# W_out and y land in the ring of keys and queries during the last pair of heads

## The chip, the cores and the metric

The kernel runs on one core of one Trainium2 chip. A core has TensorE (PE, with its weight loads listed as PEld), VectorE (DVE), ScalarE (ACT), GpSimd (POOL) and SyncE (SP), whose queue sends the DMAs of this kernel; PSUM holds the sums of matmuls, SBUF all other tiles. The metric is the device time of one execution in microseconds; lower is better. The kernel before takes 1277.64 us, the median of three runs (1276.83 to 1278.07).

## What is computed

A trunk of two layers on a sequence of 1024 tokens with 1024 channels. Layer 0 mixes by causal pooling, layer 1 by "forgetting" attention with 16 heads of 64 channels; both add a small attention into 256 memory tokens, and each ends with an output projection and a layer norm:

```python
def mixer_sublayer(x, mem, w_in, w_mem_kv, w_out, main_fn):
    h = x @ w_in
    ...
    y_main = main_fn(u_main)
    y_mem = memory_attention(q_mem, mem, w_mem_kv)
    y = jnp.concatenate([y_main * jax.nn.silu(g_main), y_mem * jax.nn.silu(g_mem)], axis=-1)
    return y @ w_out
...
    x = layer_norm(ALPHA * x + y, ln_g[layer], ln_b[layer])
```

In layer 1 `main_fn` is `softmax(q k / 8 + cum[t] - cum[s])` over the causal keys, times the values. The change lies in the last two of its 16 heads.

## The kernel before

**Precision.** A product of float32 numbers is done as three products of halves: `hi_lo` (line 138) copies a tile to its rounded high part on ScalarE and subtracts it on VectorE to get the low part; `gp_hi_lo` (144) does both on GpSimd. A matmul group is then hi*hi, hi*lo, lo*hi.

**Slabs.** `slab` (170) computes 128 channels of a projection for all tokens: 48 matmuls of 512 columns in two pieces of 24, each piece with weights of 256 KB. `split_w` (148) fetches a piece into a tile of the ring "raw" (`raw`, 113: four buffers, shared by all weight pieces) and splits it into two tiles of the ring "w" (six buffers, so three pieces). From the attention on, `low[0]` is set and GpSimd does this split.

**Attention.** `fox` (793) runs the 16 heads in pairs; `hd` is the head, `i` runs over eight query tiles, from the longest (eight blocks of keys) down to one. One turn of this loop is called a step in what follows, and in pair 7 (heads 14 and 15) the code numbers it itself: `step = b * ST + i`, 0 to 15. A step does, in this order: the logits of its tile on PE into one or two buffers of the PSUM ring "L" (`probs`, 695; GpSimd first masks the diagonal block of the head's row `R`, line 707); bias and row minimum on VectorE (715); the exponential on ScalarE (723); then for the step before it the split of the probabilities into two halves (744, 745), which a transposing DMA (754) turns; part of the filling work; the values' products of the tiles that are five steps old (`LAG`), two tiles at a time (`values`, 756); and the rest of the filling.

**Filling.** `Fill` holds generators of slab matmuls, and `pump` lets them out by the column, so that PE always has work between the dependent parts. In pair 7 the filling is four slabs of gates: pair 7's own, then `late_gate` (784) for pairs 3, 5 and 6, twelve matmuls a step. A late gate loads the pair's output `o` back from memory into the ring "R" (two buffers, shared with the rows of the heads), and GpSimd multiplies it by the gate in four parts (790) and stores it.

**Order.** PE's instructions keep the order of the program (`manual_schedule`). Those of the other engines are laid out by the framework's planner; a tile's buffer is handed out from its ring when one is free, and all semaphores are made from that. `hi_lo` with `pinned` keeps its two instructions at their place in the program. Each engine, and SP's queue too, works its instructions in order.

**The output projection.** `OutProj` (337) handles W_out as 24 pieces of [128, 512] (256 KB each), in the order of `KKS`, two neighbours sharing a pair of tiles (hi and lo) that `wtile` hands out from the rings named in `wtags` (866). `fetch(upto)` sends pieces into raw buffers, `split(upto)` splits them. Eight pieces are fetched and split in pair 7, by two lists over the 16 steps: fetched up to (0, 0, 1, 2, 3, 4, 5, 6, 6, 6, 7, 7, 7, 8, 8, 8), split up to (0, 0, 0, 1, 2, 3, 4, 5, 6, 6, 6, 6, 7, 7, 8, 8). `early` (383) brings the memory part of y (chunk 2) for the first 256 tokens through two raw buffers (sent at steps 9 and 12, split at steps 11 and 15) and then multiplies it with these eight pieces, 48 matmuls that fill the five steps of "head 16", in which only the last values are left. `rest` (395) splits pieces 8 to 23, and goes through the remaining products and the norms.

**The ring "B"** (`xy`, 539) has ten buffers of 4 KB per partition. Each pair of heads takes six of them, three to a head: its queries, its keys and the keys with halves swapped. Before, W_out's tiles in pair 7 come from "MK" (pieces 0 and 1), "V" (2 and 3) and "B" (4 to 7), and y's two halves from "B". The tiles of the exponential's input (`p` in `probs`) also come from "MK", which has four buffers.

Of the kernel before, what the change touches and what calls it, by code (L numbers as in the profile page):

```python
# [9 lines left out]
F32 = mybir.dt.float32  # L10
# [8 lines left out]
P = 128  # L19
# [4 lines left out]
NH = 512  # L24
HEADS = 16
# [46 lines left out]
def trunk_kernel(ctx, tc, x, xT, memT, win, wk, wv0, wv, wmk, wmv, wout, poolw, pscale, lng, lnb, bforget, out):  # L72
# [5 lines left out]
    nc = tc.nc  # L78
# [15 lines left out]
    def nm(tag):  # L94
        count[0] += 1
        return f"{tag}{count[0]}"

    def sb(shape, tag, bufs, dt=F32, where=None):
        return (where or pool).tile(shape, dt, tag=tag, name=nm(tag), bufs=bufs)
# [4 lines left out]
    def G(shape=(P, S), dt=F32):  # L104
        return sb(list(shape), "G", 4, dt)
# [7 lines left out]
    def raw(shape):  # L113
        return sb(list(shape), "raw", 4)
# [7 lines left out]
    def w_slots(tags, where):  # L122

        def tiles(k):
            tag, bufs = tags[k]
            if tag == "w":
                return [[wt([P, NH]) for _ in range(2)] for _ in range(2)]
            if tag == "MK":
                pair = [MK([P, 2, NH]) for _ in range(2)]
            elif tag == "PG":  # L130
                pair = [sb([P, 2, NH], "P", 4, F32R), sb([P, 2, NH], "G", 4, F32R)]
            else:
                pair = [sb([P, 2, NH], tag, bufs, F32R, where) for _ in range(2)]
            return [[t[:, j, :] for j in range(2)] for t in pair]

        return tiles

    def hi_lo(hi, lo, src, pinned=False):

        pin = tc.keep_in_program_order if pinned else lambda ins: ins  # L140
        pin(nc.scalar.copy(hi, src))  # L141
        pin(nc.vector.tensor_tensor(lo, src, hi.bitcast(F32), ALU.subtract))  # L142
# [117 lines left out]
    def gate_units(w_dram, dst, XH, XL):  # L260
        return slab(w_dram, XH, XL, lambda cols, acc: gate(acc, dst[:, cols]))
# [75 lines left out]
    class OutProj:  # L337
# [4 lines left out]
        def __init__(self, l, wtile, yd):  # L342
            self.l, self.wtile, self.yd, self.ws, self.accs = l, wtile, yd, [{}, {}], None
            self.raws, self.n = [], 0

        def fetch(self, upto):

            while self.n + len(self.raws) < upto:
                n = self.n + len(self.raws)
                r = raw([P, NH])  # L350
                nc.sync.dma_start(r, wout[self.l, n // 2 % 2, 2 * self.KKS[n // 4] + n % 2])
                self.raws.append(r)
# [27 lines left out]
                            )  # L380
                            yield NH

        def early(self, yh, yl):


            for j in range(2):
                r, two = raw([P, 2, 2 * P]), slice(2 * j, 2 * j + 2)
                nc.sync.dma_start(r, self.yd[2, :, two, : 2 * P])
                yield
                hi_lo(yh[:, two, :], yl[:, two, :], r, True)  # L390
                yield
            self.accs = self.open()
            yield from self.products(self.accs, 2, yh, yl)
# [79 lines left out]
    with tc.tile_pool(name="in0", bufs=1) as in0:  # L473
# [49 lines left out]
        wtags = [("B", 8)] * 4 + [("W", 4)] * 2 + [("MK", 4)] * 2 + [("Y", 4)] * 2 + [("PG", 0), ("w", 0)]  # L523
        out_proj = OutProj(0, w_slots(wtags, in0), y0d)
# [12 lines left out]
    with tc.tile_pool(name="in1", bufs=1) as in1:  # L537

        def xy(shape=(P, S)):
            return sb(list(shape), "B", 10, F32R, in1)  # L540

        def vt(shape, dt=F32R):
            return sb(shape, "V", 4, dt, in1)
# [121 lines left out]
        def pair_units(p):  # L665

            yield from qk_units(p)
            if p >= 2:
                u = MK([P, S], F32)
                yield from slab(wv[p - 2], XH, XL, lambda cols, acc: nc.scalar.copy(u[:, cols], acc))  # L670
            pairs[p].append(first_vs[p] if p < 2 else values_of(u))
# [18 lines left out]
        def forget_rows(hd):  # L690
            R = sb([P, S], "R", 2, F32, in1)
            nc.sync.dma_start(R, cumd[hd].partition_broadcast(P))
            return R
# [90 lines left out]
        def late_gate(pr):  # L784
            o, g = sb([P, S], "R", 2, F32, in1), G()
            nc.sync.dma_start(o, y1d[pr // 4, :, pr % 4, :])
            yield from gate_units(win[1, 12 + pr], g, XH, XL)
            for c in range(4):
                cols = slice(c * 2 * P, (c + 1) * 2 * P)
                nc.gpsimd.tensor_tensor(o[:, cols], o[:, cols], g[:, cols], ALU.mult)  # L790
            nc.sync.dma_start(y1d[pr // 4, :, pr % 4, :], o)

        def fox(following, out_proj):
            fill, past, fresh = Fill(), [None] * LAG, [None]
            gs = {}

            def gate_ahead(pr):
                gs[pr] = G()
                fill.add(gate_units(win[1, 12 + pr], gs[pr], XH, XL), SLAB)

            ahead_R = forget_rows(0)
            for hd in range(HEADS + 1):
                pr, b = divmod(hd, 2)
                if hd == HEADS:
                    fill.add(lead, SLAB)
                if hd < HEADS:
                    if b == 0:
                        o, sums = G(), sb([P, 4 * ST], "sums", 2, F32, small).rearrange("p (n b i) -> p n b i", n=2, b=2)
                        if 0 < pr < 7:
                            fill.add(pair_units(pr + 1), 3 * SLAB)  # L810
                        for ahead in {0: (0, 1), 2: (2,), 4: (4,), 7: (7,)}.get(pr, ()):
                            gate_ahead(ahead)
                            if ahead == 0:
                                fill.add(following, SLAB)
                        for late in (3, 5, 6) if pr == 7 else ():
                            fill.add(late_gate(late), SLAB)
                    R, ahead_R = ahead_R, None
                for i in range(ST if hd < HEADS else LAG):
                    tile_of = ST - 1 - i
                    ahead = sum(SHARE[i:]) + (sum(SHARE) if b == 0 else 0)  # L820
                    part = fill.left * SHARE[i] / (ahead if hd < HEADS else sum(SHARE[i:LAG]))
                    new, split = None, []

                    def inverse():
                        if fresh[0]:
                            old, k, es, of = fresh[0]
                            fresh[0] = old, k, es, inverse_of(old, k, len(es), of)

                    def behind():
                        if fresh[0]:  # L830
                            split.append(halves(*fresh[0]))
                            fresh[0] = None

                    if i == 2 and hd < HEADS - 1:
                        ahead_R = forget_rows(hd + 1)
                    if pr == 7:
                        step = b * ST + i
                        out_proj.fetch((0, 0, 1, 2, 3, 4, 5, 6, 6, 6, 7, 7, 7, 8, 8, 8)[step])
                        if step == 9:
                            lead = out_proj.early(*(xy((P, 4, 2 * P)) for _ in range(2)))  # L840
                        if step in (9, 12):
                            next(lead)
                    if hd < HEADS:
                        new = (hd, tile_of, o)
                        fresh[0] = probs(hd, tile_of, R, sums, inverse, behind)
                    else:
                        inverse()
                        behind()
                    if pr == 7:
                        out_proj.split((0, 0, 0, 1, 2, 3, 4, 5, 6, 6, 6, 6, 7, 7, 8, 8)[step], True)  # L850
                        if step in (11, 15):
                            next(lead)
                    fill.pump(part * FRAC[0])
                    for what in split:
                        turn(*what)
                    older = past[0]
                    if older and older[1] % 2 == 0:
                        values(older[0], older[1] // 2, older[2])
                        if older[0] % 2:
                            pair_out(older[0] // 2, older[1] // 2, older[2], gs.get(older[0] // 2))  # L860
                    fill.pump(part * (1 - FRAC[0]))
                    past = past[1:] + [new]
                if b or hd == HEADS:
                    fill.pump(float("inf"))

        wtags = [("MK", 4), ("V", 4)] + [("B", 10)] * 4 + [("w", 0), ("MK", 4), ("R", 2), ("V", 4), ("PG", 0), ("B", 10)]
        out_proj = OutProj(1, w_slots(wtags, in1), y1d)
        with tc.manual_schedule(engines={PE}):
            own, following = pair_units(0), pair_units(1)
# [66 lines left out]
```

## Time and profile before

The table is of the profiled execution; "busy" is time in which an engine executes.

| | us |
|---|---|
| median of the runs | 1277.64 |
| the profiled execution, its own time | 1276.2 |
| its span, first to last instruction | 1274.5 |
| PE busy | 1245.2 |
| DVE busy | 803.1 |
| ACT busy | 578.3 |
| POOL busy | 172.5 |

The page's second part shows the whole span in 40 slices. PE is at 9 tenths or more almost everywhere, and the granted clock (PEclk) too; each column is 31.9 us; pair 7 of the heads is in columns 34 to 36, head 16 in the 36th, the projection and the last norms in what follows.

```profile
PE   9999999999999999999999999999999998989997
DVE  6444766366455555376457888777878887654644
PEclk9999999999999999999999999999999999989998
```

In the profile's rows a line stands for an instruction or a group of equal ones: start (or nothing), duration, engine, line of the code, operation, tile written <- tiles read, count; in brackets the idle time before it and what ended that. "pj" is the PSUM ring of the slabs, "L" that of the logits, "O" that of the values, and a tile's name is its ring's. The rows in the prediction with a stretch of time ahead give its length and the busy time of PE, PEld, DVE, ACT and POOL with instruction counts, then the granted clock, the DMA share and GB/s.

### The profile page before, as it was taken

How to read it: one execution, taken by the hardware profiler on the slowest of the kernel's cores; microseconds unless marked ns; L12 is line 12 of the kernel's file. 1: busy time of each engine (PE TensorE's matmuls, PEld its weight loads, DVE VectorE, ACT ScalarE, POOL GpSimd, SP SyncE). 2: the span in 40 equal slices, each digit the busy share in tenths (PEclk: the TensorE clock that was granted, in tenths of full speed). 3: DMA queues.
4: the chain of work that ended last, by engine and by line, in shares of the span. 5: the costliest groups of instructions: out<-in, count | busy, mean ns of one | idle time of the engine just before them, and what ended most of it. 6: DMA issues, size and time to landing. Idle time of an engine off the chain costs nothing. (4 is left out here: it accounts for less than half of the span.)

```text
span 1274.5 us, 19683 instructions
## 1 busy us (share of the span) xinstructions
PE 1245.2 (98%) x7018; PEld 1035.8 (81%) x7018; DVE 803.1 (63%) x1901; ACT 578.3 (45%) x1273; POOL 172.5 (14%) x276
## 2 busy tenths in 40 slices
PE   9999999999999999999999999999999998989997
PEld 6888888888888888888887778887888786868885
DVE  6444766366455555376457888777878887654644
ACT  5233643242321123266226677766767776542110
POOL 0000000000000000000013334343333332420000
PEclk9999999999999999999999999999999999989998
DMA  6333543242453323254517686867968697784430
GB/s 228 103 100 100 124 120 121 83 124 86 158 200 106 103 82 126 75 125 107 161 51 189 134 194 154 187 164 181 185 156 179 158 197 169 159 232 172 166 115 34
DMA packets 267427, 178.66 MB, mean 140 GB/s; under 512 B 212288, under 2 KB 225728, under 8 KB 267328
## 3 DMA queue, kind: packets, MB, share of 16 engines
q1 hardware_dynamic: 267328, 177.40, 52.6%
q8 instruction: 55, 0.90, 0.3%
q14 instruction: 44, 0.36, 0.1%
HBM read 94.97 MB, written 22.61 MB: 92 GB/s over the span
## 5 line engine op out<-in xcount | busy, mean ns | idle before, releaser
L180 PE MATMUL pj<-A,w 128*128 128x512 f32 x2928 | 725.3, 395 | 10.8 <-POOL w L145 9.2
L180 PEld LDWEIGHTS pj<-A,w 128*128 128x128 f32 x2928 | 537.2, 189 | 114.9 <-POOL w L145 9.6
L142 DVE TENSOR_TENSOR w<-raw,w 128x512 fp32r<-128x512 f32 x106 | 73.6, 695 | 105.5 <-ACT w L141 104.6
L723 ACT ACTIVATE T<-MK,s 128x512 f32<-128x512 f32 x192 | 110.8, 577 | 51.6 <-DVE s L715 39.2
L141 ACT CAST w<-raw 128x512 fp32r<-128x512 f32 x106 | 65.7, 621 | 149.0 <-PE pj L180 102.8
L745 DVE SCALAR_TENSOR_TENSOR P<-T,s,P 128x512 f16<-128x512 f32 x192 | 111.8, 614 | 31.6 <-ACT P L744 29.7
L744 ACT ACTIVATE P<-T,s 128x512 f16<-128x512 f32 x192 | 102.7, 576 | 46.4 <-ACT T L723 17.6
L168 PE MATMUL L<-B,B 128*128 128x512 f32 (+3 forms) x384 | 91.3, 343 | 5.0 <-DVE s L715 4.7
L168 PEld LDWEIGHTS L<-B,B 128*128 128x128 f32 x384 | 70.3, 188 | 25.9 <-DVE s L715 12.7
L620 POOL MEMSET G<- 128x128 f32 x1 | 0.2, 204 | 609.5 <-DVE V L334 609.5
L168 PEld LDWEIGHTS <-V 128*128 128x128 f16 x1152 | 66.8, 100 | 19.4 <-issue 18.9
L715 DVE CUSTOM_DVE_ANT_0 MK<-L,R 128x512 f32<-128x512 f32 (+3 forms) x128 | 72.9, 570 | 11.7 <-PE L L168 8.2
L168 PE MATMUL O<-T,V 128*128 128x128 f16 x1152 | 77.7, 223 | 1.7 <-DVE G L771 1.7
L142 DVE TENSOR_TENSOR T<-T,T 128x1024 fp32r<-128x1024 f32 x23 | 28.1, 1222 | 68.2 <-PE L L377 50.4
L146 POOL TENSOR_TENSOR w<-raw,w 128x512 fp32r<-128x512 f32 x54 | 69.7, 1291 | 3.8
L141 ACT CAST T<-T 128x1024 fp32r<-128x1024 f32 x23 | 24.2, 1052 | 99.0 <-DMA T<-y0d 50.5
L707 POOL TENSOR_SCALAR_AFFINE_SELECT R<-R 128x128 f32<-128x128 f32 x128 | 41.1, 327 | 172.3 <-DVE s L715 150.0
L145 POOL TENSOR_SCALAR w<-raw 128x512 fp32r<-128x512 f32 x54 | 35.4, 656 | 143.4 <-PE pj L180 130.4
L213 PE MATMUL pj<-T,w 128*128 128x256 f32 x384 | 48.7, 284 | 0.9 <-DVE w L142 0.8
L213 PEld LDWEIGHTS pj<-T,w 128*128 128x128 f32 x384 | 47.6, 192 | 2.0 <-DVE w L142 1.3
L377 PE MATMUL pj<-B,T 128*128 128x512 f32 x186 | 46.5, 392 | 0.5 <-DVE T L142 0.5
L377 PE MATMUL L<-B,T 128*128 128x512 f32 x174 | 43.0, 391 | 0.0
(214 smaller groups left out, 1598.6 us busy)
## 6 DMA issues: line engine op xcount, KB each, us to landing
raw<-in_win_dram SPq DMA_DIRECT2D x96, 256.0 KB, 2.8
raw<-in_wout_dram SPq DMA_DIRECT2D x48, 256.0 KB, 2.9
B<-B SPq DMA_DIRECT2D x32, 256.0 KB, 3.9
R<-cumd SPq DMA_DIRECT2D x16, 512.0 KB, 4.4
y0d<-Y SPq DMA_DIRECT2D x12, 512.0 KB, 3.1
T<-y0d SPq DMA_DIRECT2D x12, 512.0 KB, 4.1
T<-y1d SPq DMA_DIRECT2D x11, 512.0 KB, 4.0
raw<-in_wmk_dram SPq DMA_DIRECT2D x16, 256.0 KB, 2.6
```

The costliest lines, as they stand in the source:

```text
L141: pin(nc.scalar.copy(hi, src))
L142: pin(nc.vector.tensor_tensor(lo, src, hi.bitcast(F32), ALU.subtract))
L146: nc.gpsimd.tensor_tensor(lo, src, hi.bitcast(F32), ALU.subtract)
L168: nc.tensor.matmul(acc, a, b, start=i == 0, stop=i == len(terms) - 1)
L180: nc.tensor.matmul(accs[n], a[:, k, :], b[:, kt, n * NH : (n + 1) * NH], start=kt == 0 and i == 0, stop=kt == KT - 1 and i == 2,)
L213: nc.tensor.matmul(acc, w[:, k, :], m[pc][:, k, :], start=pc == 0 and k == 0 and i == 0, stop=pc == 1 and k == 3 and i == 2,)
L377: nc.tensor.matmul(accs[a][nh], y[:, k, a * P : (a + 1) * P], w, start=kt == 8 and i == 0, stop=kt == 7 and i == 2,)
L707: nc.gpsimd.affine_select(R[:, qs], R[:, qs], [[-1, P]], ALU.is_ge, -NEG, base=0, channel_multiplier=1).ins
L715: nc.vector.tensor_tensor_reduce(p[:, lo:up], lg, R[:, lo:up], 1.0, top, ALU.add, ALU.min, m[:, n : n + 1])
L723: nc.scalar.activation(e, p[:, lo:up], AF.Exp, bias=top, scale=-1.0, accum_out=sums[:, n, hd % 2, i : i + 1],)
L744: nc.scalar.activation(pair[:, lo:up], e, AF.Copy, scale=r)
L745: nc.vector.scalar_tensor_tensor(pair[:, L + lo : L + up], e, r, pair[:, lo:up], ALU.mult, ALU.subtract)
```

## The change

Pieces of W_out and of y no longer go through raw buffers in pair 7.

- A new function `land` takes a float32 tile from the ring "B". `fetch_two` sends two neighbouring pieces of W_out into the two halves of one such tile, with one DMA for each piece. It is called at steps 0, 1, 5 and 11, which makes the eight pieces.
- `early` gets one such tile for all of y's chunk (512 KB) and loads it with one DMA at step 9 in place of two into raw buffers; the halves are split from it at steps 12 and 13 (before: 11 and 15).
- The list of splits is changed: piece 5 moves from step 8 to step 11, piece 6 from step 12 to 14, piece 7 from step 14 to 15.
- At the start of head 16, `fetch(12)` sends pieces 8 to 11 into raw buffers; before, `rest` did that.
- In `wtags` the first and third entry change places: pieces 0 and 1 are split into "B", pieces 4 and 5 into "MK".

```diff
+        def fetch_two(self, land):
+
+            n = self.n + len(self.raws)
+            for j in range(2):
+                nc.sync.dma_start(land[:, j, :], wout[self.l, n // 2 % 2, 2 * self.KKS[n // 4] + j])
+                self.raws.append(land[:, j, :])
+
...
-        def early(self, yh, yl):
-
-
-            for j in range(2):
-                r, two = raw([P, 2, 2 * P]), slice(2 * j, 2 * j + 2)
-                nc.sync.dma_start(r, self.yd[2, :, two, : 2 * P])
-                yield
-                hi_lo(yh[:, two, :], yl[:, two, :], r, True)
+        def early(self, y, yh, yl):
+
+
+            nc.sync.dma_start(y, self.yd[2, :, :, : 2 * P])
+            yield
+            for two in (slice(0, 2), slice(2, 4)):
+                hi_lo(yh[:, two, :], yl[:, two, :], y[:, two, :], True)
                 yield
...
+        def land(shape):
+            return sb(list(shape), "B", 10, F32, in1)
+
...
-                        out_proj.fetch((0, 0, 1, 2, 3, 4, 5, 6, 6, 6, 7, 7, 7, 8, 8, 8)[step])
+                        if step in (0, 1, 5, 11):
+                            out_proj.fetch_two(land((P, 2, NH)))
                         if step == 9:
-                            lead = out_proj.early(*(xy((P, 4, 2 * P)) for _ in range(2)))
-                        if step in (9, 12):
+                            lead = out_proj.early(land((P, 4, 2 * P)), *(xy((P, 4, 2 * P)) for _ in range(2)))
                             next(lead)
+                    if hd == HEADS and i == 0:
+                        out_proj.fetch(12)
...
-                        out_proj.split((0, 0, 0, 1, 2, 3, 4, 5, 6, 6, 6, 6, 7, 7, 8, 8)[step], True)
-                        if step in (11, 15):
+                        out_proj.split((0, 0, 0, 1, 2, 3, 4, 5, 5, 5, 5, 6, 6, 6, 7, 8)[step], True)
+                        if step in (12, 13):
                             next(lead)
...
-        wtags = [("MK", 4), ("V", 4)] + [("B", 10)] * 4 + [("w", 0), ("MK", 4), ("R", 2), ("V", 4), ("PG", 0), ("B", 10)]
+        wtags = [("B", 10), ("V", 4), ("MK", 4)] + [("B", 10)] * 3 + [("w", 0), ("MK", 4), ("R", 2), ("V", 4), ("PG", 0), ("B", 10)]
```

## The prediction

> **What bounds the kernel now.** I read the page's totals first, then who TensorE (PE) waits for, then busy time in stretches around the change.
>
> ```profile
> span 1274.5 us, 19683 instructions
> PE 1245.2 (98%) x7018; PEld 1035.8 (81%) x7018; DVE 803.1 (63%) x1901; ACT 578.3 (45%) x1273; POOL 172.5 (14%) x276
> ```
>
> PE is busy for 98% of the span, so the change can only pay in the 29 us where PE stands still, or where it runs slowly. Who it waits for, in us, times and longest:
>
> ```profile
> PE pj L180 <- POOL w L145: 9.2, 2, 5.5
> PE L L168 <- DVE s L715: 4.7, 11, 0.7
> PE O L168 <- DVE G L771: 1.7, 1, 1.7
> PE pj L377 <- DVE T L142: 0.5, 1, 0.5
> ```
>
> The first row is two waits of a gate's slab for its weights as GpSimd (POOL) splits them. Both lie in the last pair of heads, in the steps of that pair that I count as 6 and 14 (a step is one query tile of one head; it begins with its logits on PE, and pair 7 has steps 0 to 15). In stretches, with the granted clock and the DMA share and GB/s last:
>
> ```profile
> 1053.34:1076.22 22.88, 22.88 (x135) 18.92 (x134) 18.50 (x51) 16.19 (x36) 4.36 (x7) 1.00 0.66 144
> 1076.22:1089.31 13.09, 7.42 (x46) 5.58 (x44) 5.27 (x17) 4.52 (x11) 5.06 (x7) 0.74 0.76 188
> 1089.31:1115.15 25.84, 25.84 (x150) 21.40 (x148) 19.35 (x54) 17.77 (x42) 11.94 (x18) 1.00 0.75 169
> 1115.15:1126.58 11.43, 7.69 (x46) 5.84 (x45) 3.87 (x12) 3.78 (x10) 2.66 (x4) 0.70 0.97 226
> 1126.58:1146.05 19.47, 17.24 (x107) 13.73 (x106) 13.99 (x22) 11.63 (x22) 6.58 (x7) 1.00 0.74 229
> ```
>
> Rows one and three are steps 0 to 5 and 7 to 13: PE never pauses, VectorE (DVE, third figure) is busy 81% and 75%. Rows two and four are steps 6 and 14. They are long, and PE's clock is down to 0.74 and 0.70 in them; in all other rows it is 1.00. The order of time, on PE:
>
> ```profile
> 1076.22 0.40 PE L168 MATMUL L<-B,B 128*128 128x256 f32 x2
> 1082.15 3.00 PE L180 MATMUL pj<-A,w 128*128 128x512 f32 x5 [5.54 <-POOL w L145]
> 1089.31 0.33 PE L168 MATMUL L<-B,B 128*128 128x128 f32 x2
> 1115.15 0.40 PE L168 MATMUL L<-B,B 128*128 128x256 f32 x2
> 1119.15 3.00 PE L180 MATMUL pj<-A,w 128*128 128x512 f32 x5 [3.61 <-POOL w L145]
> ```
>
> Why POOL is late is seen from POOL, SyncE's queue (SP) and DVE, in that order:
>
> ```profile
> 1081.48 0.62 POOL L145 TENSOR_SCALAR w<-raw 128x512 fp32r<-128x512 f32 x1 [3.08 <-DMA raw<-in_win_dram]
> 1118.36 0.74 POOL L145 TENSOR_SCALAR w<-raw 128x512 fp32r<-128x512 f32 x1 [3.94 <-DMA raw<-in_win_dram]
> ...
> 1055.40 0.33 SPq L351 DMA_DIRECT2D raw<-in_wout_dram  x1
> 1077.46 0.38 SPq L150 DMA_DIRECT2D raw<-in_win_dram  x1
> 1108.25 5.49 SPq L754 DMA_TRANSPOSE T<-P  x2
> 1114.46 0.39 SPq L150 DMA_DIRECT2D raw<-in_win_dram  x1
> ...
> 1076.45 0.69 DVE L142 TENSOR_TENSOR MK<-raw,MK 128x512 fp32r<-128x512 f32 x1
> 1111.14 1.13 DVE L142 TENSOR_TENSOR B<-raw,B 128x512 fp32r<-128x512 f32 x1
> ```
>
> POOL waits for the weights' DMA, and SP sent that DMA late. The ring "raw" has four buffers. At 1055.40 the fourth piece of W_out takes the last one; nothing comes free until VectorE splits the first pieces, the second ending at 1077.14. At 1077.46 the gate's weights leave, 1.2 us after the step that needs them began. For step 14 the buffer comes free with the first half of y at 1112.27, and SP sends the load at 1114.46, after the transposes that stand before it in its queue. So raw buffers held by W_out and y are the cause of both waits.
>
> **The change, part by part.**
>
> *Raw buffers freed.* In pair 7 the ring then serves the gates' weights alone, eight pieces for four buffers, so a load can go as soon as POOL has split the piece four places ahead. What the two waits cost I take from the length of the steps, since the slow clock after each wait counts too. A step of this kind without a wait is put together from rows of the same work, start to start:
>
> ```profile
> 1046.98 0.40 PE L168 MATMUL L<-B,B 128*128 128x256 f32 x2
> 1047.21 1.09 PE L180 MATMUL pj<-A,w 128*128 128x512 f32 x4
> 1048.15 1.85 PE L168 MATMUL O<-T,V 128*128 128x128 f16 x30
> 1049.81 1.41 PE L180 MATMUL pj<-A,w 128*128 128x512 f32 x5
> ...
> 1062.53 1.33 PE L180 MATMUL pj<-A,w 128*128 128x512 f32 x5
> 1063.70 0.95 PE L168 MATMUL O<-T,V 128*128 128x128 f16 x14
> 1064.46 1.87 PE L180 MATMUL pj<-A,w 128*128 128x512 f32 x7
> 1066.17 0.75 PE L168 MATMUL L<-B,B 128*128 128x384 f32 x4
> ```
>
> Two logits of 256: 0.23 (1047.21 - 1046.98); five gate matmuls 1.17; thirty of the values 1.66; seven gate matmuls 1.71. Sum 4.77 us. Step 6 took 13.09 (1076.22 to 1089.31), so 8.32 too long: 5.54 of waiting and 2.78 of slow work behind it. Step 14 took 11.43: 6.66 too long, 3.61 and 3.05. **Removed: 14.98 us**, if both loads come in time. The lower end is 0.
>
> The Trainium skill ("TensorE: Matmul & The Clock Gate", Part 1) says that the clock halves after an idle window of about 3.4 us and is whole again after about 3.4 us of sustained work. Half clock for 3.4 us would cost 1.7 us behind each wait, and the sum would be 9.15 + 3.4 = 12.6, the time 2.4 us higher than mine. The rows decide: 13.09 x 0.26 and 11.43 x 0.30 are both 3.4 us of full clock lost, twice as much. That the 1.7 us in the third row of PE's waits (at 1143) left the clock at 1.00 agrees with the page's threshold.
>
> *Landings in the ring "B".* Ten buffers of 4 KB. Pair 7's queries and keys hold six, three of which come free when head 14 is done (step 7). By the diff: two pieces land at step 0 and two at step 1 (four free, two left); step 3 gives the first split two (none left); step 4 frees one, step 5 takes it; step 6 frees one; step 7 frees three; y, its two halves and the last two pieces take all four at steps 9 to 12; steps 11 and 13 free one each, and the split of step 14 takes these. Each buffer is free at least one step (3.8 us: six in the first stretch's 22.88) before it is wanted, with none to spare. Cost taken: 0. Upper end: a cast that waits here holds ScalarE's queue, with the exponentials behind it; if the first is late by a whole step, and PE feels it all, 3.8 us.
>
> *DMAs and SP.* Eight W_out loads of 256 KB remain eight, sent in pairs; y goes as one load in place of two, one issue less (0.38 us of SP in the row at 1077.46, of the same size). SP still waits for a buffer at the third landing, with transposes behind it. Probabilities are needed on PE five steps after they are made, some 15 to 19 us, so a wait of a few us is hidden; without that cover it would cost its length. Between -0.4 and +1, taken 0. The packets of steps 0 to 15 crowd into 15 us less: 1053.34 to 1126.58 has a mean share of 0.76 by the four rows, so 0.95 in 58 us; row four carried 0.97 on all queues.
>
> *The splits moved by a step or several* (pieces 5 to 7, halves of y) are the same instructions on ScalarE and VectorE (0.69 us each on VectorE, row at 1076.45): sum 0. Their cover changes: VectorE used the waits to catch up. How far behind was it?
>
> ```profile
> 1081.62 0.48 DVE L745 SCALAR_TENSOR_TENSOR P<-T,s,P 128x256 f16<-128x256 f32 x1 [0.59 <-ACT P L744]
> ```
>
> That is its last work of step 6, done at 1082.1; unstalled, PE would begin step 7 at 1076.22 + 4.77 = 1081.0. So VectorE keeps up to within a step, and the logits have two buffers. I add 0.5 us for short waits of "PE L <- DVE" (eleven of at most 0.7 us now); ends 0 and 2.
>
> *fetch(12) at head 16* sends four W_out pieces of the output projection before it starts, through raw buffers that now are free. That helps the end of this stretch:
>
> ```profile
> 1137.57 0.61 SPq L411 DMA_DIRECT2D T<-y1d  x1
> 1143.69 1.05 ACT L141 CAST T<-T 128x1024 fp32r<-128x1024 f32 x1 [0.22 <-DMA T<-y1d]
> 1146.05 1.20 PE L377 MATMUL pj<-B,T 128*128 128x512 f32 x4 [0.49 <-DVE T L142]
> ```
>
> Here y's first chunk waits on SP behind W_out pieces. Waits of 1.7 and 0.49 us could go (-2.2); but ScalarE and VectorE also lose the pause of step 14 in which they caught up. Taken 0, upper end in the third rival.
>
> **Sum.** The profiled execution took 1276.2 us (span 1274.5 and 1.7 around it). 1276.2 - 14.98 + 0.5 = 1261.7. The median of the runs lies 1.4 above the profiled one (1277.64 - 1276.2): **1263 us**.
>
> **Rivals.**
>
> *One of the two waits stays.* For: POOL works in order, and the late gates' products (L790) wait there for a DMA, with splits behind them; SP's transposes hold loads back (5.49 us for two). Against: with buffers free the loads and splits move ahead by steps, not by microseconds. If the second stays, 1263 + 6.7 = 1269.7; if the first, 1271.3.
>
> *The wait moves to head 16.* The chain of W_out pieces and y's first chunk ended at 1146.05. If it moves up by the first step's 8.3 us but not by the second's 6.7, PE arrives that much before it: 1263 + 6.7 = 1269.7, and with half a clock behind the wait up to 1272.7. For: raw buffers turn over only as fast as VectorE splits. Against: four pieces are there beforehand.
>
> *Slower: POOL is held by the late gates' own loads.* Step 9's mask stands on POOL behind L790, which waits for its o from memory:
>
> ```profile
> 1095.11 1.43 POOL L790 TENSOR_TENSOR R<-R,G 128x256 f32<-128x256 f32 x2 [7.42 <-DMA R<-y1d]
> 1098.94 0.29 POOL L707 TENSOR_SCALAR_AFFINE_SELECT R<-R 128x128 f32<-128x128 f32 x1
> 1100.77 0.85 PE L168 MATMUL L<-B,B 128*128 128x512 f32 x4
> ```
>
> The mask ends 1.5 us before PE's next logits. It happens twice (late gates 3 and 5). If crowded DMA makes each load longer than now by d, PE waits d - 1.5 and then 2.9 more at half clock. It decides at 2(d + 1.4) > 17, d above 7 us; at d = 8 the price is 18.8 and the time 1281.8. Against: the three loads of o differ by 1.5 us, while the DMA share went from 0.75 to 0.97:
>
> ```profile
> DMA to landing us min/median/max: 4.6/5.0/6.1
> ```
>
> *The change doesn't do what it says*: the landings' waits in "B" hold SP as the raw ones did, and the gates' loads behind them are as late: 1277.6. Against: the count of buffers above.
>
> **Numbers.** Forecast 0.60 (own range 1260.5 to 1266, from the ends -2.2 and +2 with about 1 of the others), one wait stays 0.14, moved to head 16 0.10, no effect 0.05, slower 0.11. A measurement here tells 0.2%, 2.6 us, from no change. All but the last two are faster: 0.84, same 0.05, slower 0.11. Range 1260 to 1272: it holds the first and nearly all of the next two.
>
> **What would show it.** Right: no wait of PE for POOL L145 in pair 7, the clock at 1.00 from step 0 to 15, in_win loads sent several us before their splits, steps 6 and 14 at about 4.8 us. Wrong: a wait over 3.6 us and a clock under 1.00 at another place (logits behind a mask, the projection's first matmul), ScalarE idle for a "B" buffer, or SP waiting long at a landing.

## The result and the profile after

The changed kernel takes 1264.44 us, the median of six runs (1261.06 to 1266.88), against 1277.86 us for the kernel before (1275.49 to 1280.29, six runs). The ratio is 0.9892, with a 95% interval of 0.9872 to 0.9912. The profiled execution took 1262.09 us with a span of 1260.4, 14.1 less than the one before.

Totals of the changed kernel's page (the code from line 345 on has moved down; L384 is the projection's matmul, L724 the row minimum, L779 and L780 the two instructions, on ScalarE and VectorE, that empty the values' PSUM buffer, here called their evacuation):

```profile
span 1260.4 us, 19678 instructions
PE 1241.2 (98%) x7018; PEld 1033.4 (82%) x7018; DVE 802.5 (64%) x1901; ACT 577.7 (46%) x1273; POOL 173.5 (14%) x276
```

The work is the same, to five instructions. What went is PE's waiting, and slow work behind it. Whom it waits for now in the whole span:

```profile
PE L L168 <- DVE s L724: 4.5, 11, 0.5
PE O L168 <- DVE G L780: 2.0, 1, 2.0
PE idle L92 <- DVE warm L89: 1.3, 1, 1.3
PE pj L180 <- ACT A L141: 1.1, 1, 1.1
PE pj L213 <- DVE w L142: 0.8, 1, 0.8
```

The row "PE pj L180 <- POOL w L145", 9.2 us before, is gone. Between 1040 and 1140 us only the wait of 2.0 us is left. In the same stretches as before (steps 0 to 5, step 6, steps 7 to 13, step 14, then head 16 up to the projection's first matmul with a new chunk of y):

```profile
1053.22:1076.10 22.88, 22.88 (x135) 18.91 (x134) 18.56 (x52) 15.64 (x35) 8.50 (x12) 1.00 0.83 194
1076.10:1080.87 4.77, 4.77 (x45) 4.05 (x44) 3.75 (x13) 4.69 (x13) 3.42 (x4) 1.00 0.86 218
1080.87:1106.71 25.84, 25.84 (x150) 21.39 (x148) 20.47 (x57) 17.76 (x42) 11.70 (x18) 1.00 0.98 226
1106.71:1111.48 4.77, 4.77 (x46) 4.05 (x45) 3.98 (x12) 3.27 (x9) 0.69 (x1) 1.00 1.02 221
1111.48:1131.07 19.59, 17.62 (x106) 14.30 (x105) 13.56 (x22) 11.83 (x23) 7.34 (x7) 0.94 0.71 217
```

Steps 6 and 14 take 4.77 us each, with the clock at 1.00. Steps 0 to 5 and 7 to 13 last as long as before to 0.01 us. The 16 steps took 73.24 us (1053.34 to 1126.58) and take 58.26 now: 14.98 less. The last row is the exception. Its clock of 0.94 over 19.59 us means that work worth 1.2 us at the full clock was lost, and PE waits there:

```profile
1122.89 0.62 ACT L141 CAST MK<-raw 128x512 fp32r<-128x512 f32 x1 [2.87 <-DMA raw<-in_wout_dram]
1126.33 0.62 ACT L141 CAST R<-raw 128x512 fp32r<-128x512 f32 x1 [2.81 <-DMA raw<-in_wout_dram]
1126.97 0.47 ACT L779 ACTIVATE G<-O,unscale 64x256 f32<-64x256 f32 x1
1128.30 0.49 PE L168 MATMUL O<-T,V 128*128 128x128 f16 x6 [1.97 <-DVE G L780]
1128.61 2.67 PE L384 MATMUL L<-B,B 128*128 128x512 f32 x6
```

These rows are ScalarE's and PE's in order of time. The values of tiles 3 and 2 are ready on PE at 1121.9, and a short ScalarE instruction (L779), with one on VectorE behind it, should empty their PSUM buffer. It stands in ScalarE's queue behind casts of W_out pieces 15 and 16, which wait 2.87 and 2.81 us for their loads. PE's last values wait for that buffer, and the six matmuls after the wait take 2.67 us where six of this form take 1.52.

The loads that were late before leave early now. SP's rows of the gates' weights in pair 7's neighbourhood:

```profile
1047.65 0.33 SPq L150 DMA_DIRECT2D raw<-in_win_dram  x1
...
1055.92 0.38 SPq L150 DMA_DIRECT2D raw<-in_win_dram  x1
...
1063.95 0.54 SPq L150 DMA_DIRECT2D raw<-in_win_dram  x1
```

The last of these is the second piece of late gate 6, wanted at step 14. It was sent at 1114.46 before, and is sent at 1063.95 now, 43 us ahead of its step. The raw buffers don't stay with the gates' weights, though: from 1071.46 on, in step 4, the planner sends pieces 8 to 11 of W_out into them, far ahead of the place where the program asks for them.

### The profile page after: what moved, and what is told of

Same layout as the page of the kernel before. It is cut to its first block, busy times and chain, and to the rows that moved or that the text cites. A ratio compares the mean times of both kernels' runs of the same rounds, so it can differ in the third digit from the quotient of the medians.

```text
span 1260.4 us, 19678 instructions
## 1 busy us (share of the span) xinstructions
PE 1241.2 (98%) x7018; PEld 1033.4 (82%) x7018; DVE 802.5 (64%) x1901; ACT 577.7 (46%) x1273; POOL 173.5 (14%) x276
## 5 line engine op out<-in xcount | busy, mean ns | idle before, releaser
L180 PE MATMUL pj<-A,w 128*128 128x512 f32 x2928 | 722.5, 394 | 1.2 <-ACT A L141 1.1
L180 PEld LDWEIGHTS pj<-A,w 128*128 128x128 f32 x2928 | 536.0, 188 | 104.1 <-ACT A L141 2.8
L724 DVE CUSTOM_DVE_ANT_0 MK<-L,R 128x512 f32<-128x512 f32 (+3 forms) x128 | 72.9, 569 | 9.8 <-PE L L168 6.8
L141 ACT CAST T<-T 128x1024 fp32r<-128x1024 f32 x23 | 24.2, 1051 | 98.4 <-DMA T<-y0d 49.9
L145 POOL TENSOR_SCALAR w<-raw 128x512 fp32r<-128x512 f32 x54 | 35.5, 658 | 136.4 <-PE pj L180 135.9
L384 PE MATMUL pj<-B,T 128*128 128x512 f32 x186 | 46.7, 395 | 0.0
L384 PE MATMUL L<-B,T 128*128 128x512 f32 x174 | 43.1, 391 | 0.0
```

Source lines behind the costliest of these rows:

```text
L180: nc.tensor.matmul(accs[n], a[:, k, :], b[:, kt, n * NH : (n + 1) * NH], start=kt == 0 and i == 0, stop=kt == KT - 1 and i == 2,)
L384: nc.tensor.matmul(accs[a][nh], y[:, k, a * P : (a + 1) * P], w, start=kt == 8 and i == 0, stop=kt == 7 and i == 2,)
L724: nc.vector.tensor_tensor_reduce(p[:, lo:up], lg, R[:, lo:up], 1.0, top, ALU.add, ALU.min, m[:, n : n + 1])
```

## The experiments

Twelve runs were made, on three chips: e1 to e4 on one, e5 to e11 on a second, e12 on a third. The time is the median of each; the kernel before took 1276.3 to 1277.4 beside them, and 1277.9 beside the changed kernel. Between executions of one kernel a step with a wait differs too: in e9, the kernel before again, step 14 took 9.26 us where it had taken 11.43.

| run | edit | us | ratio to before, 95% | step 6, step 14 |
|---|---|---|---|---|
| changed | | 1264.4 | 0.9892 (0.9872 to 0.9912) | 4.77, 4.77 |
| e1 | y through raw as before | 1264.3 | 0.9903 (0.9885 to 0.9921) | 4.77, 4.77 |
| e2 | y alone lands in B | 1273.5 | 0.9975 (0.9964 to 0.9987) | 13.36, 4.76 |
| e3 | no fetch(12) | 1263.3 | 0.9900 (0.9882 to 0.9919) | 4.77, 4.76 |
| e4 | late pieces behind the evacuations | 1264.8 | 0.9902 (0.9884 to 0.9919) | 4.77, 4.76 |
| e5, e10 | e4 and y's first chunk in P | 1260.9, 1263.0 | 0.9881 (0.9862 to 0.9901), 0.9888 (0.9870 to 0.9906) | 4.77, 4.76 and 4.77, 4.77 |
| e6 | the changed kernel again | 1264.0 | 0.9897 (0.9880 to 0.9913) | 4.76, 4.77 |
| e7 | before, two lists changed | 1272.9 | 0.9966 (0.9953 to 0.9979) | 4.77, 8.23 |
| e8 | old rings for the halves | 1264.8 | 0.9907 (0.9893 to 0.9922) | 4.77, 4.77 |
| e9 | the kernel before again | 1276.9 (one run) | | 13.83, 9.26 |
| e11 | old list of splits | 1266.2 | 0.9905 (0.9886 to 0.9924) | 4.76, 4.77 |
| e12 | e5 and later landings | 1261.3 | 0.9875 (0.9859 to 0.9892) | 4.77, 4.77 |

### Which landing does it: e1 and e2

e1 is the changed kernel with y's chunk in raw buffers again; W_out still lands in B:

```diff
-        def early(self, y, yh, yl):
+        def early(self, yh, yl):
...
+                r, two = raw([P, 2, 2 * P]), slice(2 * j, 2 * j + 2)
+                nc.sync.dma_start(r, self.yd[2, :, two, : 2 * P])
...
-                        if step in (12, 13):
+                        if step in (11, 15):
```

> The changed kernel, but y's chunk goes through two raw buffers at the old steps (sent at 9 and 12, split at 11 and 15); W_out still lands in B. Theory (raw buffers held by W_out and y make the two waits): step 6 is at 4.8 us as in the changed kernel. At step 14 y holds at most two of the four raw buffers and the gates' pieces have two, enough to run one piece ahead: wait at most 1 us, time 1264 to 1266. Rival (step 14's wait was y's doing, as the DVE row at 1112.27 had it): step 14 stays at about 11.4 us, time 1271.

e2 is the kernel before with y alone landing in B:

```diff
-                            lead = out_proj.early(*(xy((P, 4, 2 * P)) for _ in range(2)))
-                        if step in (9, 12):
+                            lead = out_proj.early(land((P, 4, 2 * P)), *(xy((P, 4, 2 * P)) for _ in range(2)))
                             next(lead)
...
-                        if step in (11, 15):
+                        if step in (12, 13):
```

> The kernel before, with y's chunk alone landing in B (split at steps 12 and 13); W_out goes through raw buffers as before. Theory: step 6 stays at 13.1 us (four raw buffers held by W_out pieces 0 to 3), step 14 falls to 4.8 us, since only W_out's pieces 6 and 7 are in the ring then: 1277.9 - 6.7 = 1271. Rival (step 14's load is late for SP's transposes that stand before it, not for a buffer): step 14 stays, 1277.9.

The two stretches of steps 6 and 14, e1 first, then e2:

```profile
1076.16:1080.93 4.77, 4.77 (x45) 4.05 (x44) 3.75 (x13) 4.69 (x13) 3.40 (x4) 1.00 0.91 220
1107.70:1112.47 4.77, 4.77 (x46) 4.05 (x44) 3.51 (x11) 3.82 (x9) 0.57 (x2) 1.00 1.06 256
```

```profile
1075.83:1089.19 13.36, 7.61 (x46) 5.78 (x45) 5.25 (x17) 4.50 (x11) 5.05 (x7) 0.74 0.74 184
1115.03:1119.79 4.76, 4.76 (x45) 4.05 (x44) 3.82 (x12) 4.24 (x11) 0.69 (x1) 1.00 1.21 252
```

In both runs the lengths of the steps came as the theory had them, not as the rival had. Step 6 is the doing of W_out alone: with W_out in raw buffers it stays at 13.36 us. Step 14's wait needed both: it is gone when either W_out or y leaves the raw ring. SP's transposes, the rival for step 14, are there in e2 as before, but the last gate's load now leaves at 1100.69, ahead of those it stood behind, and the step is whole. In time e2 missed its expectation by 2.5 us: step 14 is 6.7 us shorter than in the first profile (4.5 than in e9), the median only 2.8 us lower than the 1276.3 beside it. The profiled execution lost some of it in head 16, by a pause of PE of 2.23 us for the values' buffer and a slow clock over the 8.3 us behind it:

```profile
1136.88:1145.20 8.32, 7.89 (x25) 5.34 (x25) 4.75 (x6) 3.35 (x6) 1.96 (x2) 0.59 0.78 268
```

That is 8.32 x 0.41 = 3.4 us of full clock. Whether the other runs of e2 lost theirs in the same way is not shown.

### The order in the raw ring: e7

```diff
-                        out_proj.fetch((0, 0, 1, 2, 3, 4, 5, 6, 6, 6, 7, 7, 7, 8, 8, 8)[step])
+                        out_proj.fetch((0, 0, 1, 2, 3, 3, 3, 5, 6, 6, 6, 7, 7, 7, 8, 8)[step])
...
-                        out_proj.split((0, 0, 0, 1, 2, 3, 4, 5, 6, 6, 6, 6, 7, 7, 8, 8)[step], True)
+                        out_proj.split((0, 0, 0, 1, 2, 3, 3, 4, 5, 6, 6, 6, 7, 7, 8, 8)[step], True)
```

> The kernel before with nothing but its two lists changed: piece 3 of W_out is fetched after the second piece of late gate 3 has asked for its raw buffer (pieces 3 and 4 at step 7), and pieces 3 to 5 are split one step later. No landings in B. Theory (raw buffers go out in the order of the program, and step 6's wait is the fourth piece of W_out taking the last one): step 6 falls from 13.1 to 4.8 us without any new buffer, step 14 stays at 11.4: 1277 - 8.3 = 1269. Rival (W_out's pieces as such crowd the ring, whatever their order): the wait moves to another step, time within 2 of before.

PE in order of time, the rows with waits of that kind:

```profile
1086.50 0.73 PE L180 MATMUL pj<-A,w 128*128 128x512 f32 x2 [0.28 <-POOL w L145]
...
1105.55 1.00 PE L180 MATMUL pj<-A,w 128*128 128x512 f32 x2 [2.15 <-POOL w L145]
...
1116.63 0.73 PE L180 MATMUL pj<-A,w 128*128 128x512 f32 x2 [2.33 <-POOL w L145]
```

Step 6 is at 4.77 us with no new buffer at all, only because pieces of W_out ask later (and three are split a step later). The gate's load that left at 1077.46 in the kernel before leaves at 1056.61, where the fourth piece of W_out had gone at 1055.40. So the buffers go to who asks first in the program, and this order made the longest wait. But the ring is still shared, and waits of 2.15 and 2.33 us turn up at steps 12 and 14, where the theory had only the latter. Both sides have a part: 1272.9 us, between the 1269 of the one and no gain of the other. Taking W_out out of the ring is worth more than this better order.

### Parts that do nothing by themselves: e3, e8, e11

e3 leaves out the two lines with `fetch(12)`.

> The changed kernel without the fetch of pieces 8 to 11 at the start of head 16; the splits of the projection fetch them as before. Theory (a fetch is sent when a raw buffer is free, wherever it stands in the program): no difference, the stretch from step 15's logits to the projection's first matmul with y stays at 19.6 us within 0.5, time 1264.4 within 2. Rival (the four pieces ahead of time carry part of the gain): the stretch grows by 2 to 5 us, with a wait over 3 us and the clock at half behind it, time 1267 to 1271.

The time is the theory's. The stretch is 18.2 us (1111.75 to 1129.91), shorter than the 19.6 expected: this execution's wait in head 16 was 1.5 us and left no slow clock. The growth that the rival forecast didn't come; the pieces are sent as early without these lines, the first at 1071.56 against 1071.46, since a raw buffer is free.

e8 sets the rings of the halves back:

```diff
-        wtags = [("B", 10), ("V", 4), ("MK", 4)] + [("B", 10)] * 3 + [("w", 0), ("MK", 4), ("R", 2), ("V", 4), ("PG", 0), ("B", 10)]
+        wtags = [("MK", 4), ("V", 4)] + [("B", 10)] * 4 + [("w", 0), ("MK", 4), ("R", 2), ("V", 4), ("PG", 0), ("B", 10)]
```

> The changed kernel with the rings of W_out's halves as before (pieces 0 and 1 split into MK, 2 and 3 into V, 4 to 7 into B). Theory (the exchange of MK and B only fits the landings in; the count of B buffers allows either): no difference, 1264 within 2, steps 6 and 14 at 4.8 us. Rival (MK's two buffers, free until step 7, let VectorE and ScalarE run closer behind PE): waits of PE for VectorE's row minimum (4.5 us in all now) grow by 1 us or more in pair 7.

```profile
PE L L168 <- DVE s L724: 6.8, 13, 1.3
PE O L168 <- DVE G L780: 1.8, 1, 1.8
PE O L168 <- DMA T<-P: 1.4, 1, 1.4
```

The time is the same within the scatter. PE's waits for VectorE are 6.8 us against 4.5, and 1.1 us of that lies in pair 7, so the rival's sign is seen. But e1 (5.6) and e5 (6.0) are above 4.5 too without that edit, so it isn't settled.

e11 sets the list of splits back and sends the last landing at step 9:

```diff
-                        if step in (0, 1, 5, 11):
+                        if step in (0, 1, 5, 9):
...
-                        out_proj.split((0, 0, 0, 1, 2, 3, 4, 5, 5, 5, 5, 6, 6, 6, 7, 8)[step], True)
+                        out_proj.split((0, 0, 0, 1, 2, 3, 4, 5, 6, 6, 6, 6, 7, 7, 8, 8)[step], True)
```

> The changed kernel with the old list of splits (piece 5 at step 8, 6 at step 12, 7 at step 14) and the last landing sent at step 9 in place of 11. Theory (B has no buffer to spare): piece 6 wants two B buffers at step 12 that come free only as y's halves are split, so a cast waits on ScalarE or VectorE around steps 12 to 14 and PE feels it: 1 to 5 us, 1265 to 1269. Rival (the waits lie within the lag of five steps): no wait of PE, 1264 within 1.

PE doesn't wait in steps 12 to 14, and step 14 is at 4.77 us: the rival holds for these steps. The median of 1266.2 with an interval that overlaps the changed kernel's doesn't show a price. Its profiled execution, 1266.7 us, has pauses of 1.89 and 2.12 us outside these steps, both with a slow clock behind them (see the last section).

### What was left in head 16: e4, e5, e10

e4 puts ScalarE's evacuations of the last values ahead of the casts that wait for loads (`evac[hd, c]` is the instruction of line 779):

```diff
-        def rest(self, resid, XH, XL, dst):
+        def rest(self, resid, XH, XL, dst, last=()):
+            for upto, ins in zip((15, 16), last):
+                self.split(upto)
+                if upto == 15:
+                    with tc.issue_after(ins):
+                        self.split(16)
+                else:
+                    with tc.issue_after(ins):
+                        self.split(24)
...
+        out_proj.rest(x1, None, None, out, [evac[HEADS - 1, c] for c in (1, 0)])
```

> The changed kernel; W_out's piece 15 is split behind the evacuation of the values' second last pair of tiles on ScalarE, pieces 16 to 23 behind that of the last pair. Theory (in head 16 PE waits 1.97 us for the values' sum, since its evacuation on ScalarE stands behind a cast that waits 2.81 us for a W_out piece, and the half clock behind this wait is what is left of the forecast): the wait goes, the clock stays at 1.00 there, 2 to 3.7 us less: 1260.7 to 1262.4. Rival (the chain of W_out pieces and y's first chunk sets the projection's start anyway): PE waits as long for y's halves, time 1264.4 within 1.

```profile
PE pj L384 <- ACT T L141: 1.4, 1, 1.4
...
PE pj L384 <- DVE T L142: 0.5, 1, 0.5
```

The wait for the values' buffer is gone, and another stands in its place: y's first chunk, sent at 1121.91 and cast at 1127.86. The stretch is 18.07 us instead of 19.59, and the median is 1264.8: the rival's time. So two chains ended within 1.4 us of each other, and e5 shortens the second one as well:

```diff
+                        if i == 0:
+                            out_proj.first = sb([P, 4, 2 * P], "P", 4)
+                            nc.sync.dma_start(out_proj.first, y1d[0][:, :, : 2 * P])
...
-                src, yh, yl = T([P, 4, 2 * P], F32), T([P, 4, 2 * P]), T([P, 4, 2 * P])
-                nc.sync.dma_start(src, self.yd[c, :, :, sp * 2 * P : (sp + 1) * 2 * P])
+                src, self.first = self.first, None
+                if src is None:
+                    src = T([P, 4, 2 * P], F32)
+                    nc.sync.dma_start(src, self.yd[c, :, :, sp * 2 * P : (sp + 1) * 2 * P])
+                yh, yl = T([P, 4, 2 * P]), T([P, 4, 2 * P])
```

> As the run before with the late pieces behind the values' evacuations, and besides this y's first chunk (the one the projection starts with) lands in a buffer of the ring P at the first step of head 16 in place of a T buffer after it. Theory (with the evacuation ahead, PE waited 1.41 and 0.53 us for this chunk, sent only when T came free and 5.9 us on its way): both waits go, the stretch from step 15's logits to the projection's first matmul with y falls from 18.1 to 16.7 us, the clock stays at 1.00: about 1.5 to 2 us below the changed kernel's fast runs with the evacuation change, 1260 to 1263. Rival (the halves' T buffers, not the landing, come late): the wait for T stays, 18 us.

> The version with the late pieces behind the evacuations and y's first chunk in P, again. Theory: 1260 to 1262 in most runs, ratio to before about 0.987; head 16 at 16.8 us with no wait over 0.5. Rival (the slower one of its four runs, 1265.6, is as common as the others): median 1263 or more.

Head 16 in e4 and in e10, the stretch from step 15's logits to the projection:

```profile
1110.88:1128.95 18.07, 16.66 (x105) 13.31 (x103) 11.24 (x20) 9.00 (x18) 6.84 (x7) 1.00 0.79 237
```

```profile
1116.33:1133.02 16.69, 16.62 (x105) 13.57 (x104) 12.20 (x19) 8.90 (x17) 7.86 (x7) 1.00 0.79 233
```

The stretch is down to its matmuls, as expected. The medians are 1260.9 and 1263.0; the second is the rival's side of the second expectation. What made these executions longer lies elsewhere in them.

### A wait ahead of pair 7: e6, e9, e12

> The changed kernel itself, unedited, on the same chip as the others of this call, to see how far its runs lie apart and what differs between them: 1264 within 2; the stretch of head 16 at 19.6 us where PE's wait for the values' sum (1.97 us in the first profile) is followed by half a clock, at 18 where it is not.

This execution lasted 1264.18 us, its head 16 took 18.51 us with the clock at 1.00, and it has a row that neither first profile has:

```profile
1048.12 1.09 PE L180 MATMUL pj<-A,w 128*128 128x512 f32 x4
1051.07 1.83 PE L168 MATMUL O<-T,V 128*128 128x128 f16 x30 [1.86 <-DMA T<-P]
```

That is in the last step but one before pair 7: the values wait for their transposed probabilities. e5, e8, e10 and e11 have this wait too, with 2.3, 1.4, 2.3 and 1.9 us.

> The kernel before, unedited, once more, for its trace on this chip. Three kernels with landings showed a wait of PE for transposed probabilities (T<-P, 1.4 to 2.3 us near 1051) on the last chip, which neither first profile has. Theory (it comes with the chip or the run): the kernel before shows such a wait too, or no kernel of this call does. Rival (the landings of steps 0 and 1, sent from 1040 on, crowd the transposes): no wait for T<-P here, and one of 1 to 2.3 us in both kernels with landings of this call.

The kernel before has no such wait (its thirty values start at 1049.28 without a pause), nor has e7, which has no landings. What SP sends ahead of the transposes, e6 first and then e9:

```profile
1035.40 0.90 SPq L150 DMA_DIRECT2D raw<-in_win_dram  x2
1036.51 4.96 SPq L763 DMA_TRANSPOSE T<-P  x1
1041.52 1.04 SPq L350 DMA_DIRECT2D B<-in_wout_dram  x2
1042.65 0.38 SPq L150 DMA_DIRECT2D raw<-in_win_dram  x1
1043.16 6.66 SPq L763 DMA_TRANSPOSE T<-P  x2
```

```profile
1035.74 0.42 SPq L150 DMA_DIRECT2D raw<-in_win_dram  x1
1036.25 0.39 SPq L351 DMA_DIRECT2D raw<-in_wout_dram  x1
1036.74 5.35 SPq L754 DMA_TRANSPOSE T<-P  x1
1042.18 0.53 SPq L351 DMA_DIRECT2D raw<-in_wout_dram  x1
1042.82 4.93 SPq L754 DMA_TRANSPOSE T<-P  x2
```

Five loads of 256 KB stand before the long transposes where three stood: the B buffer of the first landing and the raw buffers of the gates' weights came free early, and the planner used both at once. e12 moves the landings back, on top of e5:

```diff
-                            out_proj.fetch_two(land((P, 2, NH)))
+                            with tc.issue_after(turned[-1]):
+                                out_proj.fetch_two(land((P, 2, NH)))
...
-            nc.sync.dma_start_transpose(pt[hd, i][:, :n, :], two[:, : n * P])
+            turned.append(nc.sync.dma_start_transpose(pt[hd, i][:, :n, :], two[:, : n * P]).ins)
```

> The version of the two runs named tail_y, and besides this each landing of two W_out pieces is queued on SP behind the last transpose that the program has sent by then; the first landing leaves some 13 us later, behind the transposes of pair 6's last heads' long tiles. Theory (the first landing, two loads of 256 KB sent in front of the long transposes at 1040, makes PE wait 1.9 to 2.3 us for T<-P in most executions, now and then with half a clock behind it): the wait for T<-P near 1051 is gone or under 0.5, median 1259 to 1261.5, and nothing new in steps 0 to 4. Rival (the gates' weights, three loads sent in the same 10 us, suffice for it): the wait stays at 1.4 us or more, median 1262 to 1263.5.

```profile
PE L L168 <- DVE s L735: 5.4, 12, 1.1
PE idle L92 <- DVE warm L89: 1.3, 1, 1.3
PE pj L180 <- ACT A L141: 0.9, 1, 0.9
PE pj L213 <- DVE w L142: 0.8, 1, 0.8
PE O L168 <- DVE G L793: 0.5, 1, 0.5
```

No wait for T<-P, and all four runs lie between 1260.29 and 1261.76, where the changed kernel's ten lie between 1261.06 and 1266.88. In e12 three loads of 256 KB, all of them gates' weights, stand before the two long transposes, and those take 4.95 us on SP where e6's took 6.66. That fits the theory, but doesn't show it. The five traces with the wait (e5, e6, e8, e10, e11) are all of one chip; e7 and e9, on the same chip, have neither the early landing nor the early gates' loads, so they don't tell the two apart. e1, e3 and e4, on another chip, send the same five loads and wait 0 to 0.5 us, as the changed kernel's first profile does: the landing alone doesn't make the wait. And e12 ran on a third chip, of which no trace with the early landing was kept. That the early landing takes part is likely; what else it needs stays open. The stretch from the step before pair 7 to step 15's logits is longer, though:

```profile
1050.87:1112.70 61.83, 61.09 (x382) 50.15 (x381) 49.95 (x138) 42.77 (x101) 23.56 (x35) 1.00 0.91 211
```

The changed kernel needs 60.56 us for it (1050.92 to 1111.48), so 1.3 us are given back in pair 7, 0.74 of them as waits of the logits for VectorE. With 1261.3 e12's median is beside e5's 1260.9 the lowest. Its ratio's interval still overlaps the changed kernel's, and those of e5 and e10, from which it differs by the landings alone, so that it is faster is not shown.

## Why the prediction was right

- **Raw buffers held by W_out and y** as the cause of both waits: shown by e1, e2 and e7. That the ring then serves the gates' weights alone is wrong, but costs nothing: pieces 8 to 11 enter it only behind the last gate's load. Against the prediction's reading, y had no sole part in step 14; W_out's leaving is enough there too.
- **The price, 14.98 us, from step lengths**: 73.24 - 58.26 = 14.98. A whole step put together from rows of other steps, 4.77, was met to 0.01. But what there was to remove differs between executions: in e9 the same two steps, 13.83 and 9.26 us, are only 13.55 too long. That the profile used was near the common case of its kernel is not shown.
- **"VectorE keeps up to within a step", 0.5 us added**: waits for it are 4.5 us against 4.7 in the whole span, and in neither first profile does one of them lie in pair 7. Nothing was to be added, and the row "eleven of at most 0.7 us" was not one of this stretch.
- **Landings in B at no cost**: right for pair 7, where PE has no wait at all. That each buffer was free a step ahead wasn't measured; the third landing, asked for at step 5, leaves at 1077.51, in step 6. e11, where the count of buffers is worse, shows no wait of PE in steps 12 to 14.
- **DMAs and SP, taken 0, upper end 1**: mis-sized. The crowding was looked for in steps 0 to 15, whose share rose to 0.83 to 1.02 and cost nothing. It came ahead of step 0, where buffers were free before their steps: five later traces have 1.4 to 2.3 us of waiting there, three of them with a slow clock behind it. The changed kernel's first profile has none.
- **Head 16, taken 0, between -2.2 and the third rival's figure**: 1.2 us longer in the profiled execution, 19.59 against 18.36 (1126.58 to 1144.94). fetch(12), named as the help there, does nothing (e3). The wait of 1.97 us is the same as before, 1.74 there, now with slow clock behind it. That can't be put down to the change: e9, the kernel before, has 1.93 us and the slow clock too, and needs 18.97 us for this stretch (1126.28 to 1145.25); e6, the changed kernel, needs 18.51.
- **The sum**: 1263 against 1264.4. The profiled execution, without the wait at 1051, took 1262.1 against the 1261.7 worked out for it. Some of this closeness is luck: the 0.5 us for VectorE didn't come, 1.2 us in head 16 did, and the excess removed is 14.98 us in one profile of the kernel before and 13.55 in the other.
- **The rivals**: none of them came in the changed kernel. The late gates' own loads, the slower one's ground, got no longer in the denser traffic: 4.6 to 5.2 us to landing against 4.6 to 6.1, and PE has no wait for masks or splits in pair 7.

## What to carry to other kernels

When a step of known make-up is too long, price the cure by the whole step's excess over the same work elsewhere in the trace: it holds the wait and the slow clock behind it. Here it was right to 0.01 us between the two first profiles; a second trace of the same kernel gave 1.4 us less, so price from more than one. In this kernel a ring that several users share is handed out in the order of the program, so a user that asks early and releases late takes it from one that is due sooner; reordering the requests cured the first wait, a second ring the sharing. And loads that no longer waited for a buffer started well ahead of their step: see what stands behind them on the queue at that earlier place.

## What was not expected of the hardware

The clock fell after much shorter pauses of PE than the 5.54 and 3.61 us of the kernel before. These are stretches of the changed kernel right after its wait of 1.97 us, and of e6 after one of 1.87 us:

```profile
1128.30:1133.00 4.70, 4.70 (x18) 3.81 (x18) 3.74 (x6) 3.56 (x6) 1.94 (x2) 0.64 0.73 243
```

```profile
1131.23:1136.00 4.77, 4.31 (x22) 3.30 (x22) 3.80 (x6) 3.49 (x6) 2.01 (x2) 1.00 0.80 240
```

The first lost 4.70 x 0.36 = 1.7 us of full clock; the second, nearly the same pause, lost nothing. In e10 a pause of 2.25 us for T<-P made the step around it 7.93 us long (4.14 in the changed kernel's first profile, without a wait) at a clock of 0.78, again 1.7 us; in e6 1.86 us made it 6.06 long at 1.00. Around the long pauses of the kernel before 3.4 us were lost, but not all of that behind them, as the prediction's reading could suggest: 7.16 us at 0.66 and 7.43 at 0.63 are 2.4 and 2.7 us lost on work, the rest fell into the pauses.

All pauses from 1.4 to 2.4 us in the fourteen traces (the first 8 us left out) give this: seven of 1.41 to 1.87 us lost nothing; ten of 1.83 to 2.28 us lost 1.7 us each; one of 2.23 us lost 3.4 (e2, shown above), and one of 2.33 us in e7 lost nothing. What followed the pause of 2.33 us in e7, and what followed one of 1.93 us in e9 that lost 1.7:

```profile
1116.63:1122.13 5.50, 4.88 (x42) 3.84 (x43) 2.62 (x4) 1.15 (x4) 2.35 (x3) 1.00 1.08 237
```

```profile
1143.05:1149.00 5.95, 5.95 (x24) 4.63 (x24) 4.94 (x7) 4.13 (x7) 2.49 (x2) 0.71 0.73 246
```

So a pause near 2 us costs either itself or itself and, as a rule, 1.7 us more; its length alone doesn't decide which. The prediction read the 1.7 us in the third row of PE's waits, at a clock of 1.00, as agreeing with the idle window of about 3.4 us that the Trainium skill ("TensorE: Matmul & The Clock Gate", Part 1) names. Against that, eleven pauses of 1.83 to 2.28 us lost clock here, and the measurement decides. Such pauses also fit the scatter of 6 us between runs of one kernel, whose mean clocks lie between 0.995 and 0.998: one such pause lies at 677 us in e5's profiled execution (1.94 us, for VectorE), far from the change. Of the slower runs themselves there are few traces, so that all of their scatter is of this kind is not shown.
